# Half sums of the normed features on GpSimd, a fifth seven-product gate tile per FFN layer, and scores issued one head ahead of attention

## The chip, the cores and the metric

The kernel runs on one core of a Trainium2 chip. The metric is device microseconds (us) of one execution; lower is better. The inputs stay in FP32 and every matmul has FP32 accuracy.

## The reference

512 tokens of width 1024 pass through two layers and a last RMSNorm. Cut to what matters:

```python
for layer in range(2):
    h = rms_norm(x, g)
    x = x + (even_mixer(h) if layer % 2 == 0 else odd_mixer(h))
    x = x + mem_cross_attention(rms_norm(x, gx), mem)     # 4 heads, 256 memory tokens
    x = x + (silu(h2 @ w_gate) * (h2 @ w_up)) @ w_down    # h2 = rms_norm(x, gf); 2816 hidden features
return rms_norm(x, g_final)

# even: z = h @ w_in, split in u (512), cq (256), ckv (128), kr (32)
#   pool part: window means of u, minus u, times a 128x128 weight per group
#   attention: 8 heads, q = norm(cq) @ w_q_up, (k, v) = norm(ckv) @ w_kv_up, rope on 32 columns,
#              s = q k^T + causal mask, p = softmax(s), o = p v
#   out = concat(pool, o) @ w_out
# odd: gate, xb = split(h @ w_in); xb = conv4(xb); r, i = sigmoid(xb @ w_r), sigmoid(xb @ w_i)
#   a = exp(-8 r softplus(-lam)); scan h[t] = a h[t-1] + sqrt(1-a^2) i xb; out = (gelu(gate) * h) @ w_out
# cross: k = (norm(mem) * g_m) @ w_k  (rows scaled by 1/rms of each memory token)
```

## The kernel before, in words

Features lie on the 128 partitions, tokens along the free dimension: x is eight tiles of 128x512. Every FP32 operand is split into a high and a low part in fp32r (`split`, L151-161: a copy on ScalarE, L157, then a subtraction on VectorE, L158), and a product is made of three matmuls, wh·xh, wh·xl, wl·xh (`mm3`, L164-173). So one k-block of a 128x512 output is three matmuls of 512 columns, and TensorE (PE) is what the kernel is built around. Weights arrive by DMA in blocks of 512 KB into two buffers, and are split into four buffers of high and four of low parts (L115-117; casts at L102 on ScalarE, L103 on VectorE). Outputs go to eight PSUM banks under four names with two banks each: mm, att, s, tr (L47).

The stages follow each other: setup, even layer, cross attention, FFN, odd layer, cross attention, FFN, tail. Each engine works through its own queue in order; the order in the queues comes from the framework's scheduler, which runs over the whole program. `issue_after` makes an instruction come behind another one in that order.

**Even layer** (L441-650). `qkv_pair(p)` makes q for two heads (bank att, times a rotary row on VectorE, L545, then split) and k. `attend(h, ...)` makes, for one head, four rows of scores in banks s (L581-584, the mask added by a matmul), a softmax per row (`softmax_row`, L652-658: maximum on VectorE, exponential and scaling on ScalarE, into tiles pr), transposes into banks tr (L596), splits them (pth, ptl) and multiplies them with v into a bank att (L611). The pairs are written so that q and k of the next pair stand ahead of both heads of this pair; behind each pair come two tiles of the memory keys of layer 0 (`mem_keys`, named mg, xk in the profile; eight tiles of 24 matmuls of 128x256, L377-386) and one pool tile (evp, pp). The key tile leaves its bank by a VectorE product with the row Rmem (L386). Weights of q, k (evqkv) and v (evv) have three pools of one buffer each, apart from the common ones.

**Odd layer** (L940-1077). Convolution tiles and recurrent gates come first, then the scan on VectorE and ScalarE (`lru_scan`, tiles h). While that runs, PE makes the gate tiles 0 to 3 (odin weights, 24 matmuls of 128x512 each), key tiles 0 to 3 of the memory of layer 1, gate tiles 4 to 7, key tiles 4 to 7, all in the two mm banks. A gate tile leaves its bank by a VectorE product with the row Rrow (L1053), a key tile by one with Rmem (L386).

**FFN** (L770-938). 22 gate tiles f in five parts; when a part is done, its down product is made piece by piece behind the next part's tiles (`down`, bank s, 12 matmuls of 512 columns for four k-blocks; two pieces per tile f, L913-917). In a plain tile f, 8 k-blocks of gate and of up make 48 matmuls of 128x512. The tiles f = 0, 1 use x times its gain and are scaled by the row R behind the product; meanwhile `normed` (L794-803) makes normed features in four buffers (tag sraw), which the plain tiles from f = 2 on use in split form. From f = 5 on a tile is made by `fast` (L819-869): seven products of half sums, of four k-blocks each, make the two 128x512 outputs, 84 matmuls of 128x256. The half sums of the weights (sa, sb, from the raw weights gr) are made per tile on VectorE; those of the features (ta, tb) once per layer in `halves` (L805-817), four operations of 128x256 for each of four k, L810-813, all on VectorE, followed by splits. These use temporaries of tag t2, of which there are two. The raw weights gr of the fast tiles use the same four sraw buffers as the normed features, so the first ones wait for `halves` to have read them.

Of the kernel before, what the change touches and what calls it, by code (L numbers as in the profile page):

```python
# [9 lines left out]
F32 = mybir.dt.float32  # L10
# [4 lines left out]
ALU = mybir.AluOpType  # L15
# [3 lines left out]
P = 128  # L19
T = 512  # L20
D = 1024
KD = D // P
NT = T // P
MEM = 256
# [11 lines left out]
FAST = range(5, 20), range(5, 22)  # L36
# [71 lines left out]
class Trunk:  # L108
# [268 lines left out]
    def mem_keys(self, layer, mg, m0, m1, low=None):  # L377
# [4 lines left out]
        for m in range(m0, m1):  # L382
# [3 lines left out]
            self.nc.vector.tensor_mul(self.keys[:, m, :], ps[:, :MEM], self.Rmem)  # L386
# [54 lines left out]
    def even(self, nrm, nxt_spec):  # L441
# [4 lines left out]
        with ExitStack() as ctx:  # L446
# [8 lines left out]
            wsm = [ctx.enter_context(tc.tile_pool(name=f"evw{i}", bufs=1)) for i in "rhl"]  # L455
# [80 lines left out]
            Wqkv = Weights(self, ins["ev_qkv"], "evqkv", wsm)  # L536
# [32 lines left out]
            def attend(h, q, k, yh, yl):  # L569
                qh, ql = q  # L570
                kh, kl = k
                pr = [pt.tile([P, (i + 1) * P], F32, name=self.nm("pr"), tag=f"pr{i}", bufs=1 if i == 2 else 2) for i in range(NT)]
                for grp in ((0, 1), (2,), (3,)):
# [3 lines left out]
                    for i in grp:  # L577
# [6 lines left out]
                        nc.tensor.matmul(s[:, o + n - P:o + n], self.identb, self.maskb, start=False, stop=True)  # L584
                        reg[i] = r
                        o += n
                    for i in grp:
                        self.softmax_row(reg[i], pr[i])
                tiles = {}
# [17 lines left out]
                for j in range(NT):  # L607
                    vh, vl = (a[:, hp] for a in vs[j])
                    o = ps[:, j * P:]
                    th, tl = tiles[j]  # L610
                    nc.tensor.matmul(o, vh, th, start=j == 0, stop=False)  # L611
                    nc.tensor.matmul(o, vh, tl, start=False, stop=False)
                    nc.tensor.matmul(o, vl, th, start=False, stop=j == NT - 1)
# [10 lines left out]
            def att_pair(p, q, k):  # L624
                y = self.pair(YS)
                for i in range(2):
                    attend(2 * p + i, q[i], k[i], *y)
                y_att.append(y)

# [3 lines left out]
            qkv = qkv_pair(0)  # L633
            for p in range(HEADS // 2):
                q, k = qkv
                if p == 0:
                    v_tiles()
                qkv = qkv_pair(p + 1) if p + 1 < HEADS // 2 else None
                att_pair(p, q, k)
                if p == 0:  # L640
                    mg = self.mem_gained(0, self.xp, "x")
                else:
                    self.mem_keys(0, mg, 2 * p - 2, 2 * p)
                pool_tile(p, us[p])
# [603 lines left out]
```

## Time and profile before

| | |
|---|---|
| time, median of 3 runs | 1379.61 us (1379.57 to 1381.86) |
| profiled execution | 1381.9 us, its span 1379.9 us, mean granted clock 0.992 |
| PE busy | 1354.2 us, 98% of the span |
| VectorE (DVE), ScalarE (ACT) busy | 953.3 us (69%), 665.5 us (48%) |
| GpSimd (POOL) busy | 110.0 us (8%), 122 instructions |
| DMA | 139.41 MB, mean 101 GB/s |

Busy is the sum of the stretches in which at least one instruction of the engine ran. The groups of instructions show the busy time of a group, its mean duration, and the idle time of the engine just before its instructions with what ended it. A group's durations overlap on PE, since matmuls are pipelined; what one costs in the stream is the distance between two starts. PEclk in a window is the granted TensorE clock, 1.00 being full speed. The stretches used below are the even layer's attention (about 56 to 165 us), the FFN of layer 0 around its tiles 3 to 8 (about 356 to 453 us) and the odd layer's gate and key tiles (about 740 to 830 us).

### The profile page before, as it was taken

To read this page: it belongs to the slowest core of one execution; us is meant where nothing else is said; L and a number is where in the kernel's file an instruction comes from. 1 tells how busy PE (TensorE), PEld (TensorE's weight loads), DVE (VectorE), ACT (ScalarE), POOL (GpSimd) and SP (SyncE) were. 2 spreads that over 40 slices of the span, in tenths; PEclk is the share of its full clock that TensorE was granted. 3 is DMA by queue.
4 is the path that set the end of the run, shared out by engine and by line. 5 is a ranking of instruction groups with operands and counts; after the bars stand their busy time and mean duration, and the time that the engine had idled before them with its cause. 6 is when DMAs were issued, how large, how long until landed. Compare 5 with 4: busy or idle time off the path is not lost.

```text
span 1379.9 us, 19407 instructions
## 1 busy us (share of the span) xinstructions
PE 1354.2 (98%) x7640; PEld 1183.3 (86%) x7640; DVE 953.3 (69%) x1488; ACT 665.5 (48%) x1073; POOL 110.0 (8%) x122
## 2 busy tenths in 40 slices
PE   9899999999999999999999989999999999999998
PEld 8678788888889999999888878888888999999987
DVE  7787573455787777777888587435549777777643
ACT  8478653354444444444535655335445344444431
POOL 0231021013000000000110001111120000000001
PEclk9899999999999999999999999999999999999999
DMA  7221262323243323321332334223324223233131
GB/s 248 67 92 41 73 194 81 103 81 103 78 142 107 106 94 98 112 93 43 116 111 83 104 107 139 100 68 92 109 99 142 93 93 108 92 107 108 37 117 62
DMA packets 44971, 139.41 MB, mean 101 GB/s; under 512 B 5584, under 2 KB 9808, under 8 KB 44880
## 3 DMA queue, kind: packets, MB, share of 16 engines
q1 hardware_dynamic: 43440, 136.86, 30.6%
q10 hardware_dynamic: 1440, 1.32, 0.3%
q8 instruction: 60, 0.98, 0.3%
q14 instruction: 31, 0.25, 0.1%
HBM read 135.93 MB, written 2.10 MB: 100 GB/s over the span
## 4 chain that ended last, share of the span: by engine, by line
PE 90%; DVE 5%; ACT 3%; issue 1%; POOL 0%; POOLq 0%; DVEq 0%; ACTq 0%
PE mm L171 15%; PE mm L172 15%; PE mm L173 15%; PE s L171 6%; PE s L173 6%; PE s L172 6%; PE att L171 6%; PE att L172 6%; PE att L173 6%; PE tr L172 1%; PE tr L173 1%; PE tr L171 1%; PE tr L188 1%; DVE xk_l L103 1%; PE att L688 1%
## 5 line engine op out<-in xcount | busy, mean ns | idle before, releaser
L171 PE MATMUL s<-act,dn_h 128*128 128x512 f32 x304 | 119.2, 393 | 0.5 <-DVE x L279 0.5
L172 PE MATMUL s<-act,dn_h 128*128 128x512 f32 x304 | 118.8, 391 | 0.6 <-DVE act L158 0.6
L173 PE MATMUL s<-act,dn_l 128*128 128x512 f32 x304 | 114.6, 393 | 0.0
L157 ACT CAST sw_h<-gr 128x1024 fp32r<-128x1024 f32 x64 | 53.4, 835 | 105.8 <-PE att L172 58.2
L251 POOL TENSOR_TENSOR ssq<-ssq,t 128x512 f32<-128x512 f32 x30 | 50.7, 1690 | 615.1 <-ACT t L250 615.1
L158 DVE TENSOR_TENSOR sw_l<-gr,sw_h 128x1024 fp32r<-128x1024 f32 x64 | 61.3, 958 | 17.6 <-ACT sw_h L157 14.6
L172 PE MATMUL mm<-tb,sw_h 128*128 128x256 f32 x256 | 72.5, 283 | 0.0
L173 PE MATMUL mm<-tb,sw_l 128*128 128x256 f32 x256 | 72.3, 283 | 0.0
L171 PE MATMUL mm<-tb,sw_h 128*128 128x256 f32 x256 | 71.8, 280 | 0.0
L157 ACT CAST sw_h<-sb 128x1024 fp32r<-128x1024 f32 x32 | 33.5, 1048 | 75.4 <-PE s L172 67.8
L171 PEld LDWEIGHTS s<-act,dn_h 128*128 128x128 f32 x304 | 57.3, 189 | 11.3 <-DVE x L279 0.9
L172 PEld LDWEIGHTS s<-act,dn_h 128*128 128x128 f32 x304 | 57.1, 188 | 11.3 <-DVE act L158 1.0
L279 DVE TENSOR_TENSOR x<-s,x 128x512 f32<-128x512 f32 x72 | 49.5, 687 | 23.6 <-PE s L173 23.6
L173 PEld LDWEIGHTS s<-act,dn_l 128*128 128x128 f32 x304 | 57.2, 188 | 10.0
L103 DVE TENSOR_TENSOR dn_l<-dn_raw,dn_h 128x1024 fp32r<-128x1024 f32 (+1 forms) x40 | 46.8, 1171 | 16.0 <-ACT dn_h L102 15.9
L102 ACT CAST dn_h<-dn_raw 128x1024 fp32r<-128x1024 f32 (+1 forms) x40 | 40.3, 1007 | 31.1 <-ACT pc L854 17.0
L279 DVE TENSOR_TENSOR x<-mm,x 128x512 f32<-128x512 f32 x24 | 16.4, 691 | 51.4 <-PE mm L173 51.4
L102 ACT CAST gu_h<-gu_raw 128x1024 fp32r<-128x1024 f32 x24 | 25.3, 1053 | 55.3 <-PE mm L172 37.7
L157 ACT CAST sw_h<-sa 128x1024 fp32r<-128x1024 f32 x32 | 33.6, 1051 | 34.9 <-PE mm L172 33.4
L173 PE MATMUL mm<-act,xq_l 128*128 128x512 f32 x128 | 50.1, 391 | 0.0
L172 PE MATMUL mm<-act,xq_h 128*128 128x512 f32 x128 | 50.0, 390 | 0.0
L171 PE MATMUL mm<-act,xq_h 128*128 128x512 f32 x128 | 49.9, 390 | 0.0
(478 smaller groups left out, 4509.9 us busy)
## 6 DMA issues: line engine op xcount, KB each, us to landing
gr<-in_ffn_gu_dram SPq DMA_DIRECT2D x64, 512.0 KB, 3.5
dn_raw<-in_ffn_down_dram SPq DMA_DIRECT2D x32, 512.0 KB, 3.5
gu_raw<-in_ffn_gu_dram SPq DMA_DIRECT2D x24, 512.0 KB, 3.5
xk_raw<-in_xa_w_k_dram SPq DMA_DIRECT2D x16, 512.0 KB, 3.5
xq_raw<-in_xa_w_q_dram SPq DMA_DIRECT2D x16, 512.0 KB, 3.5
xv_raw<-in_xa_w_v_dram SPq DMA_DIRECT2D x16, 512.0 KB, 3.5
xo_raw<-in_xa_w_o_dram SPq DMA_DIRECT2D x16, 512.0 KB, 3.5
odin_raw<-in_od_w_in_dram SPq DMA_DIRECT2D x16, 512.0 KB, 3.5
```

The source lines that it names most:

```text
L102: nc.scalar.copy(hi, src)
L103: self.low.tensor_sub(lo, src, hi[:, :].bitcast(F32))
L157: a = nc.scalar.copy(hi, src)
L158: b = nc.vector.tensor_sub(lo, src, hi.bitcast(F32))
L171: nc.tensor.matmul(out, wh, xh, start=begin and i == 0, stop=False, **kw)
L172: nc.tensor.matmul(out, wh, xl, start=False, stop=False, **kw)
L173: self.mm_ins = nc.tensor.matmul(out, wl, xh, start=False, stop=end and i == last, **kw).ins
L188: self.sum_ins = nc.tensor.matmul(ps[:, o + t:o + t + 1], a[:, t * P:(t + 1) * P], self.ones[:, 0:1], start=i == 0, stop=i == len(terms) - ...
L251: (low or nc.gpsimd).tensor_add(ssq[:, :n], ssq[:, :n], sq[:, :n])
L279: self.nc.vector.tensor_add(self.x[m], ps, self.x[m] if src is None else src)
L688: nc.tensor.matmul(banks[t], a[:, ts], wh[:, ws], start=k == 0, stop=False)
```

## The change

Five edits come together.

1. `FAST` starts at f = 4 in both layers: one tile per layer goes from plain to fast, and it is the first one that uses the half sums.
2. In `halves` the four operations per k go from VectorE to GpSimd, and b gets the other sign; `fast` makes sb with the other sign to match.
3. Key tiles of layer 1 leave the bank by a copy on ScalarE; the product with Rmem is made in place on VectorE in the cross attention, ahead of the split of that tile.
4. Gate tiles 4 to 7 leave the bank by a copy on ScalarE; the product with Rrow follows in place on VectorE.
5. `attend` is cut in two, `scores` (score matmuls and softmax) and `attend` (transposes, splits, product with v). The scores of head h+1 are issued ahead of `attend` of head h, and the products with v are held behind the last score matmul. The row tile pr2 gets two buffers instead of one, and the evqkv weights use the common weight buffers in place of their own.

```diff
-FAST = range(5, 20), range(5, 22)
+FAST = range(4, 20), range(4, 22)
...
-            self.nc.vector.tensor_mul(self.keys[:, m, :], ps[:, :MEM], self.Rmem)
+            if layer == 0:
+                self.nc.vector.tensor_mul(self.keys[:, m, :], ps[:, :MEM], self.Rmem)
+            else:
+                self.nc.scalar.copy(self.keys[:, m, :], ps[:, :MEM])
...
-            Wqkv = Weights(self, ins["ev_qkv"], "evqkv", wsm)
+            Wqkv = Weights(self, ins["ev_qkv"], "evqkv")
...
-                        nc.tensor.matmul(s[:, o + n - P:o + n], self.identb, self.maskb, start=False, stop=True)
+                        self.score_ins = nc.tensor.matmul(s[:, o + n - P:o + n], self.identb, self.maskb, start=False, stop=True).ins
...
-                for j in range(NT):
...
+                with tc.issue_after(self.score_ins):
+                    for j in range(NT):
...
-            def att_pair(p, q, k):
-                y = self.pair(YS)
-                for i in range(2):
-                    attend(2 * p + i, q[i], k[i], *y)
-                y_att.append(y)
...
+            pair_of(0)
+            v_tiles()
+            pr = scores(0, *heads[0])
+            for h in range(HEADS):
+                p = h // 2
+                if h % 2 == 0:
+                    y = self.pair(YS)
+                    y_att.append(y)
+                    if p + 1 < HEADS // 2:
+                        pair_of(p + 1)
+                nxt_pr = scores(h + 1, *heads[h + 1]) if h + 1 < HEADS else None
+                attend(h, pr, *y)
+                pr = nxt_pr
+                if h % 2:
...
+                    pool_tile(p, us[p])
...
+                key = self.keys[:, m, :]
+                if layer:
+                    nc.vector.tensor_mul(key, key, self.Rmem)
+                self.split(key, h, l)
...
-                nc.vector.tensor_sub(a[:, lo], g[0][:, lo], g[0][:, hi])
-                nc.vector.tensor_sub(a[:, hi], g[1][:, hi], g[0][:, hi])
-                nc.vector.scalar_tensor_tensor(b[:, lo], a[:, lo], -1.0, g[1][:, hi], op0=ALU.mult, op1=ALU.subtract)
-                nc.vector.scalar_tensor_tensor(b[:, hi], b[:, lo], -1.0, g[1][:, lo], op0=ALU.mult, op1=ALU.subtract)
+                nc.gpsimd.tensor_sub(a[:, lo], g[0][:, lo], g[0][:, hi])
+                nc.gpsimd.tensor_sub(a[:, hi], g[1][:, hi], g[0][:, hi])
+                nc.gpsimd.tensor_add(b[:, lo], a[:, lo], g[1][:, hi])
+                nc.gpsimd.tensor_sub(b[:, hi], b[:, lo], g[1][:, lo])
...
-            nc.vector.tensor_add(sb[:, :T], sa[:, :T], w11)
-            nc.vector.tensor_add(sb[:, T:], sb[:, :T], w12)
+            nc.vector.scalar_tensor_tensor(sb[:, :T], sa[:, :T], -1.0, w11, op0=ALU.mult, op1=ALU.subtract)
+            nc.vector.tensor_sub(sb[:, T:], w12, sb[:, :T])
...
-                nc.vector.tensor_mul(t, ps, self.Rrow)
+                if m < KH:
+                    nc.vector.tensor_mul(t, ps, self.Rrow)
+                else:
+                    nc.scalar.copy(t, ps)
+                    nc.vector.tensor_mul(t, t, self.Rrow)
```

The number of PE matmuls goes from 7640 to 7712, 36 more in each FFN layer. The order of the instructions on the engines changes at these places. First the even layer, PE's queue of the kernel before, where the score matmuls of a head (s) end, and its transposes (tr, of the rows pr) and products with v (att from pth, vh) follow; cqh, evqkv is a q tile of the next pair:

```order
383 L583 MATMUL s_1113<-act_100_539,act_93_532 128x384
384 L584 LDWEIGHTS identb
385 L584 MATMUL s_1113<-maskb,identb 128x128
386 L596 MATMUL tr_924<-ident,pr_876 128x128
387 L596 MATMUL tr_933<-ident,pr_876 128x128
388 L611 MATMUL att_949<-pth_929,vh_716 128x512
389 L171 MATMUL att_1054<-cqh_426,evqkv_h_1050 128x512
```

In the changed kernel the same stretch of PE's queue:

```order
383 L603 MATMUL tr_966<-ident,pr_827 128x128
384 L603 MATMUL tr_975<-ident,pr_827 128x128
385 L171 MATMUL mm_1386<-pp_1382,evp_h_657 128x512
386 L172 MATMUL mm_1386<-pp_1383,evp_h_657 128x512
387 L173 MATMUL mm_1386<-pp_1382,evp_l_658 128x512
388 L584 MATMUL s_954<-act_100_530,act_92_522 128x512
389 L585 MATMUL s_954<-act_101_531,act_92_522 128x512
390 L586 MATMUL s_954<-act_100_530,act_93_523 128x512
391 L587 LDWEIGHTS identb
392 L587 MATMUL s_954<-maskb,identb 128x128
393 L619 MATMUL att_991<-pth_971,vh_707 128x512
```

The last row of scores and a pool tile now stand between the last transposes of a head and its product with v.

Second the odd layer, DVE's queue of the kernel before, at the first key tile (the product into keys at L386), in the middle of the scan (h, i):

```order
890 L1040 SCALAR_TENSOR_TENSOR h_7171<-t_1261_8154,h_7171 128x512
891 L103 TENSOR_TENSOR xk_l_7861<-xk_raw_7858,xk_h_7860 128x1024
892 L386 TENSOR_TENSOR keys_6780<-mm_7768,Rmem 128x256
893 L1040 SCALAR_TENSOR_TENSOR h_7214<-t_1262_8158,h_7214 128x512
894 L1044 TENSOR_TENSOR i_7288<-h_7128,i_7288 128x512
```

In the changed kernel that bank is emptied from ACT's queue (L389), where the table load of the square roots, square roots (L1012), squares (L1057) and the cast of a gate weight (odin_h) stand ahead of it:

```order
631 L1012 ACT_TABLE_LOAD
632 L1012 ACTIVATE h_7176<-h_7176 128x512
633 L1057 ACTIVATE t_1278_8214<-r_7396 128x512
634 L1012 ACTIVATE h_7219<-h_7219 128x512
635 L102 CAST odin_h_7940<-odin_raw_7938 128x1024
636 L389 COPY keys_6828<-mm_7816 128x256
637 L1057 ACTIVATE t_1279_8218<-r_7509 128x512
638 L1012 ACTIVATE h_7262<-h_7262 128x512
639 L389 COPY keys_6828<-mm_7848 128x256
```

The emptying of the first key tile has moved from behind a weight split on DVE to behind the table load, three instructions of the scan and a weight cast on ACT. The sixteen operations of `halves` in a layer now stand as one run in POOL's queue.

More of the change, by code (lines that the diff above doesn't have):

```diff
@@ L454, in even @@
             pt = ctx.enter_context(tc.tile_pool(name="evpt", bufs=2))
-            wsm = [ctx.enter_context(tc.tile_pool(name=f"evw{i}", bufs=1)) for i in "rhl"]
             z, zins = self.z, self.mm_ins
@@ L567, in v_tiles, with scores @@
                     vs.append((h, l))
-            def attend(h, q, k, yh, yl):
+            def scores(h, q, k):
                 qh, ql = q
                 kh, kl = k
-                pr = [pt.tile([P, (i + 1) * P], F32, name=self.nm("pr"), tag=f"pr{i}", bufs=1 if i == 2 else 2) for i in range(NT)]
+                pr = [pt.tile([P, (i + 1) * P], F32, name=self.nm("pr"), tag=f"pr{i}", bufs=2) for i in range(NT)]
                 for grp in ((0, 1), (2,), (3,)):
@@ L588, in attend @@
                         self.softmax_row(reg[i], pr[i])
+                return pr
+            def attend(h, pr, yh, yl):
                 tiles = {}
@@ L606, in attend @@
                 hp = slice(h // 2 * P, (h // 2 + 1) * P)
-                for j in range(NT):
[L608 to L613, printed above, removed]
+                with tc.issue_after(self.score_ins):
+                    for j in range(NT):
+                        vh, vl = (a[:, hp] for a in vs[j])
+                        o = ps[:, j * P:]
+                        th, tl = tiles[j]
+                        nc.tensor.matmul(o, vh, th, start=j == 0, stop=False)
+                        nc.tensor.matmul(o, vh, tl, start=False, stop=False)
+                        nc.tensor.matmul(o, vl, th, start=False, stop=j == NT - 1)
                 rs = slice((h % 2) * VD, (h % 2 + 1) * VD)
@@ L632, in even, with pair_of @@
             wph, wpl = Weights(self, ins["ev_pool"], "evp").get(0)
[L633 to L644, printed above, removed]
+            heads = []
+            def pair_of(p):
+                q, k = qkv_pair(p)
+                heads.extend(zip(q, k))
+            pair_of(0)
[12 more added lines that the diff above has]
+                if h % 2:
+                    if p == 0:
+                        mg = self.mem_gained(0, self.xp, "x")
+                    else:
+                        self.mem_keys(0, mg, 2 * p - 2, 2 * p)
+                    pool_tile(p, us[p])
             self.mem_keys(0, mg, 6, KD)
@@ L674, in k_tile @@
                 l = kvp.tile([P, MEM], F32R, name=self.nm("kl"), tag=f"kl{m}")
-                self.split(self.keys[:, m, :], h, l)
+                key = self.keys[:, m, :]
+                if layer:
+                    nc.vector.tensor_mul(key, key, self.Rmem)
+                self.split(key, h, l)
                 return h, l
@@ L1052, in gate_tile @@
                 t = self.actp.tile([P, T], F32, name=self.nm("g"), tag=f"act{other}")
-                nc.vector.tensor_mul(t, ps, self.Rrow)
+                if m < KH:
+                    nc.vector.tensor_mul(t, ps, self.Rrow)
+                else:
+                    nc.scalar.copy(t, ps)
+                    nc.vector.tensor_mul(t, t, self.Rrow)
                 return t
```

## The prediction

> **What bounds the kernel now.** I read the page first, then the groups of instructions with the idle time in front of them, then windows and the timeline around each edited place. From the page:
>
> ```profile
> PE 1354.2 (98%) x7640; PEld 1183.3 (86%) x7640; DVE 953.3 (69%) x1488; ACT 665.5 (48%) x1073; POOL 110.0 (8%) x122
> PE 90%; DVE 5%; ACT 3%; issue 1%; POOL 0%; POOLq 0%; DVEq 0%; ACTq 0%
> ```
>
> PE is busy for 98% of the span and holds 90% of the chain that ended last. So the change can gain in three ways only: fewer matmul columns, fewer waits of PE, and less time at a reduced clock behind such waits. The groups on PE whose idle time the edits touch (the last columns: busy time and mean ns, then idle time before, by releaser):
>
> ```profile
> L171 PE MATMUL mm<-act,odin_h 128*128 128x512 f32 x112 | 44.5, 398 | 3.5 <-DVE g L1053 2.8 <-DVE keys L386 0.7
> L171 PE MATMUL mm<-mg,xk_h 128*128 128x256 f32 x128 | 36.9, 288 | 1.9 <-DVE keys L386 1.9
> L596 PE MATMUL tr<-ident,pr 128*128 128x128 f32 x80 | 16.1, 279 | 2.0 <-ACT pr L658 1.6 <-DVE ptl L158 0.3
> L611 PE MATMUL att<-pth,vh 128*128 128x512 f32 x8 | 3.6, 444 | 2.4 <-ACT pth L157 2.4
> L581 PE MATMUL s<-act,act 128*128 128x512 f32 x8 | 3.4, 431 | 0.7 <-ACT pr L656 0.5
> ```
>
> Three stages are edited, and PE's idle time in their edited waits is about 5 us in the odd layer, 5 us at the heads of the attention, and two waits at its beginning.
>
> **FFN: a fast tile for f = 4.** The windows give one plain tile (48 matmuls of 512 columns) and one fast tile with its two down pieces (84 of 256 columns and 24 of 512); after start, end and length come the busy times of PE, PEld, DVE, ACT and POOL, then PEclk:
>
> ```profile
> 391.10:402.00 10.90, 10.90 (x50) 9.03 (x49) 9.60 (x16) 4.63 (x8) 0.00 (x0) 1.00 0.58 188
> 437.10:452.70 15.60, 15.60 (x110) 14.58 (x109) 12.20 (x17) 6.95 (x10) 0.00 (x0) 1.00 0.30 102
> ```
>
> 10.90 / 48 = 0.227 us per 512-column matmul. The fast tile alone is 15.60 − 24 × 0.227 = 10.15 us. So each layer saves 10.90 − 10.15 = 0.75 us, two layers **1.5 us**, if the half sums are there in time. They come from Pool now. The timeline has the normed features and before's last TB split:
>
> ```profile
> 360.90 5.39 DVE L799 SCALAR_TENSOR_TENSOR xn<-x,vecs,R 128x512 f32<-128x512 f32 x8
> 399.92 0.69 DVE L158 TENSOR_TENSOR tb<-t,tb 128x512 fp32r<-128x512 f32 x1
> ```
>
> and the groups with Pool's nearest operations, and VectorE's one that is replaced:
>
> ```profile
> L251 POOL TENSOR_TENSOR ssq<-ssq,t 128x512 f32<-128x512 f32 x30 | 50.7, 1690 | 615.1 <-ACT t L250 615.1
> L548 POOL TENSOR_TENSOR act<-t,act 128x512 fp32r<-128x512 f32 x6 | 7.9, 1318 | 38.6 <-ACT act L547 38.6
> L1097 POOL TENSOR_TENSOR t<-t,t 128x384 f32<-128x384 f32 x6 | 6.1, 1013 | 326.9 <-ACT t L1095 326.9
> L810 DVE TENSOR_TENSOR t<-xn 128x256 f32<-128x256 f32 x8 | 3.3, 418 | 0.0
> ```
>
> No row has Pool at 256 columns. The two quicker rows differ by 305 ns for 128 columns, 2.38 ns per column, which puts 256 columns at 0.71 us; half of the slowest row gives 0.85. Before's last TB split ran at 399.92, which was early enough, since the first fast tile began at 402.0. Now it begins at 391.1. Its products run X·f1 and Y·f2 first, from features that are ready long before; with 12 matmuls of 10.15 / 84 = 0.121 us a product is 1.45 us, so TA is needed from 394.0 and TB from 395.5. Pool can begin after the fifth of the eight normed tiles, 360.9 + 5 × 0.67 = 364.3. It makes a and b of one k in 4 × 0.71 = 2.9 us, and must then wait until VectorE has split them, because there are two t2 buffers. VectorE still has the weight splits of f = 2, 3 and 5 to do between. Walking the new orders of VectorE and Pool row by row, the last TA is split at about 387 and the last TB at about 392: 7 and 4 us ahead of need. What hides the sixteen operations is thus 27 us of plain tiles; if VectorE fell 4 us behind, every further us would come straight out of the 1.5. Bounds of the term: 1.5 down to −2.5 (the cover gone by 2 us in each layer). I take 1.5. The Trainium skill, "GPSIMD Engine Reference", section 4.1 on engine selection, advises VectorE for ordinary elementwise work, with Pool about half as fast; that agrees with 0.71 against 0.418 here, and by the rule the edit is a loss if it matters at all, which is the third rival.
>
> In the fast tiles sb costs nothing: DVE is busy 12.20 of 15.60 there.
>
> **Odd layer: banks emptied by ScalarE.** The timeline of before where the four odin and key tiles meet:
>
> ```profile
> 784.75 0.28 PE L171 MATMUL mm<-mg,xk_h 128*128 128x256 f32 x1
> 795.12 0.36 PE L171 MATMUL mm<-mg,xk_h 128*128 128x256 f32 x1 [1.57 <-DVE keys L386]
> 798.97 0.47 PE L171 MATMUL mm<-act,odin_h 128*128 128x512 f32 x1 [0.75 <-DVE keys L386]
> 818.36 0.47 PE L171 MATMUL mm<-act,odin_h 128*128 128x512 f32 x1 [2.78 <-DVE g L1053]
> 825.49 0.28 PE L171 MATMUL mm<-mg,xk_h 128*128 128x256 f32 x1
> ```
>
> and the window behind its last wait:
>
> ```profile
> 815.00:826.00 11.00, 8.22 (x32) 6.41 (x31) 7.62 (x10) 2.70 (x4) 0.00 (x0) 0.84 0.47 144
> ```
>
> The three waits are 1.57 + 0.75 + 2.78 = 5.1 us. Behind the last one, 24 matmuls took 825.49 − 818.36 = 7.13 us where 24 × 0.227 = 5.45 is usual, at a granted clock of 0.84 in that window: about 1.65 more. Price of what is touched: 6.75 us. The release by VectorE goes, because it came late there: scans of h fill its queue. What is late next is ScalarE:
>
> ```profile
> 788.53 1.28 ACT L994 ACT_TABLE_LOAD   x1
> 789.83 0.63 ACT L994 ACTIVATE h<-h 128x512 f32<-128x512 f32 x1
> 790.36 0.62 ACT L1039 ACTIVATE t<-r 128x512 f32<-128x512 f32 x1
> 790.88 0.62 ACT L994 ACTIVATE h<-h 128x512 f32<-128x512 f32 x1
> 791.41 1.03 ACT L102 CAST odin_h<-odin_raw 128x1024 fp32r<-128x1024 f32 x1
> 789.16 0.42 DVE L386 TENSOR_TENSOR keys<-mm,Rmem 128x256 f32<-128x256 f32 x1
> ```
>
> with a copy of that size from the groups:
>
> ```profile
> L854 ACT COPY pc<-mm 128x256 f32<-128x256 f32 x32 | 11.7, 365 | 2.0 <-PE mm L173 2.0
> ```
>
> In the new order the copy of the first key tile stands behind just these five ACT instructions. The first bank was free at 789.58 before; now the copy starts behind the cast, at 791.41 + 1.03 = 792.4, and ends near 792.75 (0.365 for one of 128x256). The third key tile takes that bank. It began without a wait at 795.12 − 1.57 − 2.9 = 790.65 (the fourth tile's start, less its wait, less the 24 × 0.121 us of the third), so it would now wait about 2.1 us. The later copies follow in an ACT queue with more slack; I allow 0.75 in all, for a cast that waits for its DMA ahead of one copy. So the term is 6.75 − 2.1 − 0.75 = **3.8 us**. Bounds: 2.3, if the new wait brings a slow clock as the 2.78 one did (−1.5), and 5.0 if ACT runs ahead of the walk. The product in place adds 8 × 0.42 us to VectorE in the cross attention, and 4 × 0.68 behind gate tiles; neither holds a bank of PE. Behind the latter wait the gelus, which come after the whole scan in ACT's queue.
>
> **Even layer: scores a head ahead.** Its beginning:
>
> ```profile
> 65.27 0.68 DVE L545 TENSOR_TENSOR t<-att,ropeC 128x512 f32<-128x512 f32 x1
> 66.00 0.50 PE L171 MATMUL att<-evv_h,ckh 128*128 128x512 f32 x1 [2.83 <-DVE t L545]
> 69.41 0.47 PE L582 MATMUL s<-act,act 128*128 128x128 f32 x1 [1.33 <-DVE act L158]
> 57.99 1.21 DVE L103 TENSOR_TENSOR xk_l<-xk_raw,xk_h 128x1024 fp32r<-128x1024 f32 x1
> ```
>
> and the window behind the first wait:
>
> ```profile
> 66.00:76.00 10.00, 8.18 (x28) 5.72 (x28) 7.69 (x17) 4.33 (x8) 3.57 (x3) 0.66 0.36 111
> ```
>
> The first wait, 2.83 us, is for the rotary product that empties the bank of head 1's q. In VectorE's new order one xk split (1.21) leaves the way to it and two operations of 0.68 (a split of evv's weight and one of a pool tile) come in: 0.15 us later. The second wait, 1.33, loses about 1.0: the splits of 1.21 and 0.68 that stood ahead of the low half of k are gone, and one of about 0.8 is new. The waits at the heads are those of the groups above: L596 for pr 1.6, L611 for pth 2.4, L581 for pr 0.5, together 4.5. In the new order 12 score matmuls of the next head, and often a pool or key tile, stand ahead of the transposes; head 7 has no next head, and the ends of pairs were already filled by q and key tiles. I take two thirds, 3.0. Sum: 3.0 + 1.0 − 0.15 = **3.85 us**. Bounds: 7.05 if all 4.5 go and half of the 3.4 us that a clock of 0.66 costs in 10 us goes too; −1.0 if the shared weight buffers cost a cast and a split, 1.05 + 1.21, once or twice on the path. The 1.05 is the cast of a 128x1024 weight:
>
> ```profile
> L102 ACT CAST gu_h<-gu_raw 128x1024 fp32r<-128x1024 f32 x24 | 25.3, 1053 | 55.3 <-PE mm L172 37.7
> ```
>
> **Sum**: 1.5 + 3.8 + 3.85 = 9.15 us. The profiled execution is 1381.9 us (span 1379.9 and 2.0 outside it), 2.3 above the median of 1379.61; it would come to 1372.8, and the median to 1370.5 us. About 0.2%, 2.8 us, is what a measurement can tell from no change: faster is below 1376.9, slower above 1382.4.
>
> **The rivals.**
>
> *The attention gains only at its beginning.* Before's PE order already lets the scheduler put q tiles and key tiles between the products with v, so what waits at the heads may be the softmax chain itself, maximum to exponential to scale, which is as long in the new order. For it: ACT ends 2.4 + 1.6 of these waits and stays as loaded. Against it: the scores now come a whole head earlier. Even gives 1.0 in place of 3.85: 1373.3.
>
> *The new key copy wait brings a slow clock.* A wait of 2.83 was followed by a window at 0.66, one of 2.78 by 0.84; the one of 1.57 was not. The new one, 2.1, lies between. Price 1.5: 1372.0. The Trainium skill, "TensorE: Matmul & The Clock Gate", Part 1, has the clock fall only after an idle window of about 3.4 us; the two waits here were shorter, so the measurement decides, and by the page this rival would not exist.
>
> *The half sums on Pool lie on the path.* If PE waits for TA and TB at f = 4, the sixteen operations cost 16 × (0.71 − 0.418) = 4.7 us a layer, 9.3 in two: 1379.8, no change. Against it stands the slack of 4 us in the walk.
>
> *The weight buffers starve the key tiles (slower).* evqkv and evv take places in the common high and low buffers, of which there are four, while pool weights hold one for the whole attention. If two q, k weights are held at once, key tiles get one buffer, and each waits for its cast and split behind the tile before, 1.05 + 1.21 = 2.26 us. Their raw blocks take turns in the two raw buffers as well, and SP issues the DMAs in order. Over the six key tiles inside the attention: 13.6 us, 1370.5 + 13.6 = 1384.1. It turns the sign from (1379.6 − 1370.5) / 6 = 1.5 us per tile, and passes 1382.4 from 2.0. Against it: a q, k weight is read by 15 matmuls and is then free, and VectorE and ACT have idle time in the attention.
>
> **How the numbers follow.** My forecast 0.50, first rival 0.17, second 0.10, third 0.07, fourth 0.06; the remaining 0.10 is better than forecast, the slow clock at the attention's beginning gone too (−3.4, 1367.1). The range 1364.5 to 1377.0 takes in the sum of the upper bounds (7.05 − 3.85 and 5.0 − 3.8 give 4.4; with the other half of that clock, 1.7, it is 6.1) and of the lower ones (2.3 and −1.0 in place of 3.8 and 3.85 give 6.35). Faster 0.85: all of forecast, first, second and better, less 0.02 for two lower bounds at once; same 0.09; slower 0.06.
>
> **What would show it.** Right: in the changed profile no wait of PE on L1053's bank from gate tile 4 on; a wait of about 2 us, released by ACT's copy, at the third key tile of layer 1; the first fast tile of a layer in about 10.15 us with no idle time in front of the TA and TB products; less than 2 us of idle time at the transposes and products with v. Wrong: idle time of PE behind Pool or a TB split near 394; waits at mg, xk tiles in the attention, released by xk casts or splits; a granted clock below 0.9 in other stretches than before.

## The result, and the profile after

The changed kernel takes 1390.26 us (median of 4 runs, 1389.09 to 1391.59); beside it the kernel before took 1380.48 (1379.57 to 1381.86). The ratio is 1.0067, with a 95% interval of 1.0055 to 1.0080: slower, where 1370.5 was forecast and 1377.0 was the upper end of the range. The profiled execution has 1391.14 us and a span of 1389.4, 9.5 us more than before's profiled one.

The first matmul with the weights of each stage, in the timelines of the two profiles, gives the length of the stages (us). "FFN 1" ends here where its plain tile f = 20 begins.

| stage | before | changed | difference | predicted |
|---|---|---|---|---|
| even, first evqkv to first xq | 153.8 | 154.1 | +0.3 | −3.85 |
| FFN 0, first gu to first odin | 346.1 | 351.2 | +5.1 | −0.75 |
| odd, first odin to first odout | 145.2 | 143.7 | −1.5 | −3.8 |
| FFN 1, first gu to f = 20 | 294.0 | 298.9 | +4.9 | −0.75 |

The rest of the 9.5 is −0.5 ahead of the even layer, +0.1 in the cross attention and +1.1 at the very end, nearly all behind the last instruction that issues an output DMA.

The engines' row of the changed kernel's page (compare 1354.2, 953.3, 665.5 and 110.0 before):

```profile
PE 1356.1 (98%) x7712; PEld 1190.1 (86%) x7712; DVE 964.6 (69%) x1476; ACT 675.5 (49%) x1095; POOL 153.4 (11%) x154
```

Pool has 43 us more for 32 operations, where 32 × 0.71 = 23 were reckoned. VectorE is busy for 11 us more: the two fast tiles give it sums and splits, but 32 operations of 0.42 us have left it. The groups on PE that answer to those shown of before, with the idle time in front of them:

```profile
L171 PE MATMUL mm<-act,odin_h 128*128 128x512 f32 x112 | 43.7, 390 | 0.0
L171 PE MATMUL mm<-mg,xk_h 128*128 128x256 f32 x128 | 38.4, 300 | 9.0 <-DVE act L161 5.0 <-ACT keys L389 2.1 <-ACT g L1074 1.9
L603 PE MATMUL tr<-ident,pr 128*128 128x128 f32 x80 | 15.0, 282 | 1.8 <-ACT pr L673 1.2 <-DVE ptl L158 0.6
L619 PE MATMUL att<-pth,vh 128*128 128x512 f32 x8 | 3.9, 486 | 0.0
L584 PE MATMUL s<-act,act 128*128 128x512 f32 x8 | 3.5, 438 | 0.0
```

The waits that the change is aimed at are gone: 3.5 to 0 at gate tiles, 2.4 to 0 at the product with v, 2.0 to 1.8 at the transposes. In their place the key tiles wait 9.0 us instead of 1.9, for three releasers that before did not have. And a new place waits, the first fast tile of each FFN layer; PE's timeline of layer 0:

```profile
396.05 0.38 PE L171 MATMUL mm<-tb,sw_h 128*128 128x256 f32 x1 [0.64 <-ACT pc L872]
398.10 0.39 PE L172 MATMUL mm<-tb,sw_h 128*128 128x256 f32 x1 [0.59 <-DVE tb L158]
400.90 0.50 PE L171 MATMUL s<-act,dn_h 128*128 128x512 f32 x1 [2.30 <-ACT dn_h L102]
```

and the windows around them (columns as above: PE, PEld, DVE, ACT, POOL busy, PEclk, DMA):

```profile
391.00:402.00 11.00, 7.48 (x53) 6.67 (x52) 11.00 (x16) 6.11 (x11) 2.73 (x3) 0.98 0.39 119
402.00:407.00 5.00, 5.00 (x28) 4.69 (x27) 4.11 (x7) 1.68 (x2) 0.00 (x0) 0.70 0.47 161
```

PE idles 3.5 of 11 us there, VectorE not at all (11.00 of 11.00), and behind it the clock is at 0.70 for 5 us (3.4 us at 0.50, so 1.7 us lost). These two make up about the 5.1 us of FFN 0: the 0.75 that the fast tile saves is used up by matmuls that start at longer distances just behind each wait (0.8 in all). TB is late, and the casts that follow are late with it. How the half sums ran, from Pool's timeline:

```profile
373.56 3.53 POOL L828 TENSOR_TENSOR t<-xn 128x256 f32<-128x256 f32 x1 [5.37 <-DVE ta L158]
377.05 2.38 POOL L829 TENSOR_TENSOR t<-xn 128x256 f32<-128x256 f32 x1
379.39 0.73 POOL L830 TENSOR_TENSOR t<-t,xn 128x256 f32<-128x256 f32 x1
381.37 1.19 POOL L828 TENSOR_TENSOR t<-xn 128x256 f32<-128x256 f32 x1
384.48 0.75 POOL L831 TENSOR_TENSOR t<-t,xn 128x256 f32<-128x256 f32 x1
...
388.26 1.12 POOL L828 TENSOR_TENSOR t<-xn 128x256 f32<-128x256 f32 x1 [3.04 <-DVE ta L158]
389.35 1.72 POOL L829 TENSOR_TENSOR t<-xn 128x256 f32<-128x256 f32 x1
391.81 1.60 POOL L830 TENSOR_TENSOR t<-t,xn 128x256 f32<-128x256 f32 x1 [0.74 <-DVE tb L158]
393.49 1.06 POOL L831 TENSOR_TENSOR t<-t,xn 128x256 f32<-128x256 f32 x1
```

and from VectorE's and ScalarE's:

```profile
388.71 1.76 DVE L158 TENSOR_TENSOR sw_l<-gr,sw_h 128x1024 fp32r<-128x1024 f32 x1
390.99 0.67 DVE L158 TENSOR_TENSOR tb<-t,tb 128x512 fp32r<-128x512 f32 x1
392.73 1.23 DVE L158 TENSOR_TENSOR ta<-t,ta 128x512 fp32r<-128x512 f32 x1
397.37 0.68 DVE L158 TENSOR_TENSOR tb<-t,tb 128x512 fp32r<-128x512 f32 x1
...
399.28 0.62 ACT L157 CAST act<-t 128x512 fp32r<-128x512 f32 x1 [3.28 <-DVE t L893]
399.80 1.04 ACT L102 CAST dn_h<-dn_raw 128x1024 fp32r<-128x1024 f32 x1
```

With VectorE idle beside it an operation takes 0.73 to 0.75 us, as the sum had it (0.71). Beside a working VectorE it takes 1.06 to 1.21, and up to 3.53 where VectorE runs splits and one product without a pause, each in its usual 0.68. VectorE pays too: a split of 0.67 takes 1.23, one of 1.21 takes 1.76. The Trainium skill, "SBUF — State Buffer", section "Who interferes with whom", says that a VectorE instruction with two inputs in SBUF contends with a GpSimd instruction that reads SBUF, through a shared read interface; this trace agrees: thirteen of the sixteen operations of layer 0 are lengthened, VectorE's own beside some of them too, with the prices given here.

The last TB split ends at 398.05 where the walk had 392. Two in-order queues carry this on: VectorE's product for tile f = 3 (L893) stands behind that split, ScalarE's cast of that product behind it, and the cast of the down weights behind that, so the down product waits 2.30 us for an engine that was idle for 3.28.

### The profile page after: what moved, and what is told of

Read it like the earlier page. It is cut to its first block, busy times and chain, and to the rows that moved or that the text cites. A ratio compares the mean times of both kernels' runs of the same rounds, so it can differ in the third digit from the quotient of the medians.

```text
span 1389.4 us, 19596 instructions
## 1 busy us (share of the span) xinstructions
PE 1356.1 (98%) x7712; PEld 1190.1 (86%) x7712; DVE 964.6 (69%) x1476; ACT 675.5 (49%) x1095; POOL 153.4 (11%) x154
## 5 line engine op out<-in xcount | busy, mean ns | idle before, releaser
L157 ACT CAST sw_h<-gr 128x1024 fp32r<-128x1024 f32 x68 | 56.7, 834 | 102.6 <-PE att L172 55.3
L172 PE MATMUL mm<-tb,sw_h 128*128 128x256 f32 x272 | 77.2, 284 | 1.2 <-DVE tb L158 1.2
L158 DVE TENSOR_TENSOR sw_l<-gr,sw_h 128x1024 fp32r<-128x1024 f32 x68 | 66.2, 973 | 17.4 <-ACT sw_h L157 14.1
L171 PE MATMUL mm<-tb,sw_h 128*128 128x256 f32 x272 | 76.5, 281 | 1.1 <-ACT pc L872 1.1
L173 PE MATMUL mm<-tb,sw_l 128*128 128x256 f32 x272 | 76.9, 283 | 0.0
L171 PEld LDWEIGHTS mm<-tb,sw_h 128*128 128x128 f32 x272 | 51.7, 190 | 1.6 <-ACT pc L872 1.5
L172 PEld LDWEIGHTS mm<-tb,sw_h 128*128 128x128 f32 x272 | 51.0, 188 | 1.7 <-DVE tb L158 1.6
L173 PEld LDWEIGHTS mm<-tb,sw_l 128*128 128x128 f32 x272 | 51.1, 188 | 0.0
```

Of the source, the lines that this page charges most:

```text
L157: a = nc.scalar.copy(hi, src)
L158: b = nc.vector.tensor_sub(lo, src, hi.bitcast(F32))
L171: nc.tensor.matmul(out, wh, xh, start=begin and i == 0, stop=False, **kw)
L172: nc.tensor.matmul(out, wh, xl, start=False, stop=False, **kw)
L173: self.mm_ins = nc.tensor.matmul(out, wl, xh, start=False, stop=end and i == last, **kw).ins
```

## The experiments

Stages of the runs, in us as in the table above, with times and ratios to the kernel before on the same chip. A dash is a stage that the run does not edit.

| run | even | FFN 0 | odd | FFN 1 | median us | ratio (95% interval) |
|---|---|---|---|---|---|---|
| f4_only | – | 347.1 | – | 295.1 | 1384.38 | 1.0021 (1.0009 to 1.0033) |
| pool_halves_only | – | 346.1 | – | 294.0 | 1381.42 | 1.0003 (0.9993 to 1.0012) |
| two_k_on_gpsimd | – | 349.1 | – | 296.7 | 1385.07 | 1.0032 (1.0021 to 1.0044) |
| early_tile_third_buffer | – | 351.8 | – | 297.8 | 1392.83 | 1.0098 (1.0080 to 1.0116) |
| attn_only | 153.5 | – | – | – | 1380.87 | 0.9998 (0.9989 to 1.0008) |
| attn_own_weights | 151.7 | – | – | – | 1377.97 | 0.9982 (0.9972 to 0.9992) |
| changed_own_weights | 151.7 | 351.2 | 143.9 | 300.3 | 1389.05 | 1.0054 (1.0038 to 1.0070) |
| key_copies_only | – | – | 142.5 | – | 1378.34 | 0.9987 (0.9977 to 0.9998) |
| gate_copies_only | – | – | 142.0 | – | 1378.37 | 0.9981 (0.9972 to 0.9991) |
| without_ffn_edits | 151.7 | – | 142.1 | – | 1373.80 | 0.9959 (0.9945 to 0.9973) |
| first_key_on_vector | 150.2 | – | 139.4 | – | 1372.17 | 0.9935 (0.9921 to 0.9948) |

The unedited stages tell how far a stage can be trusted: the FFN layers lay within 0.1 us of 346.1 and 294.0 in every run that left them alone; the odd layer came out at 145.0 to 145.2 or at 143.6, the even layer at 153.8 in before and 155.2 to 156.0 in six runs. The steps are stretches in which PE runs at half clock (granted clock 0.50), as the last section shows. So in the even and odd columns a difference of 1.7 or 3.4 us can be the clock alone.

**f4_only: the early tile without Pool.**

```diff
-FAST = range(5, 20), range(5, 22)
+FAST = range(4, 20), range(4, 22)
```

> The kernel before with the first edit alone: f = 4 becomes a fast tile in both layers, the half sums stay on VectorE. Theory A (VectorE's queue is what is late at f = 4: in about 385 to 402 us it was busy for 11.00 of 11.00 us, because the sums and the splits of the first fast tiles' weights fall on the end of the half sums, and GpSimd only makes it a little worse): PE waits at the first fast tile of each layer here too, 3 us or more with a slow clock behind it, and each FFN layer gets longer than in the kernel before, by 2 to 7 us; total 1384 to 1394. Theory B (the half sums are late because GpSimd is slow, 1.06 to 3.53 us an operation): with VectorE's 0.42 the TA and TB products do not wait, each layer gets 0.75 shorter; total about 1379.

FFN 0 took 347.1 and FFN 1 295.1, 1.0 and 1.1 above before. TB does not make PE wait in f = 4, though its last split ran as late as 401.42 (this FFN begins 1.6 us later than the changed kernel's); here the scheduler has put the last three TB matmuls behind a product and 20 matmuls of the down pieces. VectorE's split and PE's next wait in the two timelines:

```profile
401.42 0.68 DVE L158 TENSOR_TENSOR tb<-t,tb 128x512 fp32r<-128x512 f32 x1
...
398.71 0.29 PE L173 MATMUL mm<-tb,sw_l 128*128 128x256 f32 x1
404.82 0.28 PE L171 MATMUL mm<-tb,sw_h 128*128 128x256 f32 x1
405.94 0.39 PE L171 MATMUL mm<-act,sw_h 128*128 128x256 f32 x1 [0.57 <-ACT sw_h L157]
```

What is left is a ripple of small waits (0.57, 0.22, 0.23) at the second fast tile, whose weights are split late; with the matmuls that start late just behind them (0.8 in all) they cost 1.8, less the saving of 0.75. So each theory gets a part: theory B is right that Pool makes most of the loss (5.1 and 4.9 against 1.0 and 1.1), theory A that the early tile loses even without it. The saving of 0.75 is there (48 matmuls of 0.227 go, 84 of 0.12 come), but it is used up.

**pool_halves_only: Pool without the early tile.**

```diff
-                nc.vector.tensor_sub(a[:, lo], g[0][:, lo], g[0][:, hi])
+                nc.gpsimd.tensor_sub(a[:, lo], g[0][:, lo], g[0][:, hi])
...
```

> The kernel before with the second edit alone: half sums on GpSimd, fast tiles from f = 5 as before. Theory A: the sixteen operations have 16 us more until the first fast tile needs them, and VectorE has 16 x 0.42 = 6.7 us less to do; no wait of PE at the first fast tile, the time as before within 0.1% (1379 to 1381). Theory B, if GpSimd is so slow that it is late even then: waits at the first TA or TB product, 1 to 4 us a layer, total 1382 to 1388.

346.1 and 294.0, as before, with no wait at the first fast tile. Pool's operations are just as long as in the changed kernel:

```profile
374.60 3.54 POOL L810 TENSOR_TENSOR t<-xn 128x256 f32<-128x256 f32 x1 [5.37 <-DVE ta L158]
380.43 0.74 POOL L812 TENSOR_TENSOR t<-t,xn 128x256 f32<-128x256 f32 x1
394.52 1.07 POOL L813 TENSOR_TENSOR t<-t,xn 128x256 f32<-128x256 f32 x1
```

So neither edit alone explains the loss: 0.0 for one, 1.0 for the other, 5.1 for both. Sixteen us more cover hide the slow operations altogether. VectorE's busy time shows what they cost it:

```profile
PE 1353.6 (98%) x7640; PEld 1183.2 (86%) x7640; DVE 952.1 (69%) x1456; ACT 665.7 (48%) x1073; POOL 152.5 (11%) x154
```

It lost 32 operations of 0.42 us, 13.4 in all, and got 1.2 us back (953.3 to 952.1).

**two_k_on_gpsimd: half of the half sums on Pool.**

```diff
-                nc.vector.tensor_sub(a[:, lo], g[0][:, lo], g[0][:, hi])
+                eng = nc.gpsimd if k < 2 else nc.vector
+                eng.tensor_sub(a[:, lo], g[0][:, lo], g[0][:, hi])
...
```

> The first and second edits (fast tile at f = 4), but GpSimd makes the half sums of k = 0 and 1 only and VectorE those of k = 2 and 3. Theory H (what is late is the second half of GpSimd's run, which lies beside VectorE's full queue at 380 to 398 us, where both engines slow each other): each FFN layer is between 0.75 us below and 1.1 us above before (346.1 and 294.0 us), as with all half sums on VectorE, instead of 5.1 and 4.9 above; total 1379 to 1383. Theory I (any half sums on GpSimd make VectorE's operations beside them long, 1.23 for 0.68, and that alone makes the first fast tile late): 2 us or more above before in each layer, total 1384 to 1390.

2.9 and 2.7 above before: theory I by the number, though the run does not separate longer operations from the new order of the queues. The loss of FFN 0 grows with the operations on Pool: 1.0 with none, 2.9 with eight, 5.1 with sixteen, of which 1.7 is the half clock that neither of the others has; 3.4 without it. PE now waits for TA as well as TB:

```profile
394.05 0.38 PE L172 MATMUL att<-ta,sw_h 128*128 128x256 f32 x1 [0.99 <-DVE ta L158]
397.03 0.39 PE L171 MATMUL mm<-tb,sw_h 128*128 128x256 f32 x1 [0.48 <-ACT tb L157]
404.59 0.38 PE L171 MATMUL mm<-act,sw_h 128*128 128x256 f32 x1 [0.67 <-ACT sw_h L157]
```

**early_tile_third_buffer: a buffer more between the two engines.**

```diff
-                a, b = self.tmp("t2"), self.tmp("t2")
+                a, b = self.tmp("t2"), st.tile([P, T], F32, name=self.nm("t"), tag="th", bufs=1)
```

> The first and second edits (fast tile at f = 4, half sums on GpSimd), with a buffer of its own for b beside the two t2 temporaries for a, so that GpSimd can go on with the next k while VectorE splits the last. In the changed kernel GpSimd waited 5.4, 3.0 and 0.7 us a layer for VectorE's splits of ta and tb, and its sixteen operations took 21.4 us. Theory G (the waits between the two engines make the half sums late): the last TB split comes 2 us or more earlier, the waits of 0.6 + 0.6 + 2.3 us at the first fast tile shrink to under 1 us, and an FFN layer is back at the 346.1 us of before or below. Theory B (each operation is long because VectorE works at the same time, 1.06 to 3.53 us against 0.73 alone): the waits shrink by less than half, each FFN layer stays 2 us or more above before; total 1384 to 1390.

Theory G falls: 5.7 (with 1.7 of half clock) and 3.8 (with none) above before; the total, 1392.83, is even above theory B's 1384 to 1390. The last TB split came at 395.57, 0.9 us earlier than in the changed kernel when both are counted from the first gu matmul, and PE waited longer, 3.62 us. The reason is in ScalarE's queue:

```profile
394.92 0.62 ACT L157 CAST tb<-t 128x512 fp32r<-128x512 f32 x1 [2.50 <-POOL t L813]
398.10 0.62 ACT L157 CAST act<-t 128x512 fp32r<-128x512 f32 x1 [2.04 <-DVE t L875]
398.62 0.37 ACT L854 COPY pc<-mm 128x256 f32<-128x256 f32 x1
```

PE needed the copy pc (L854), which empties the bank for the TB product. It stood behind a cast that waited for VectorE, which itself had waited 1.28 us for ScalarE's cast of the late half sum. The late half sum had itself taken 3.38 us on Pool. So a late Pool operation held up both in-order queues, and what PE missed is a copy that has nothing to do with half sums.

**attn_only: scores a head ahead.** The fifth edit alone, cut to its core:

```diff
-            Wqkv = Weights(self, ins["ev_qkv"], "evqkv", wsm)
+            Wqkv = Weights(self, ins["ev_qkv"], "evqkv")
...
+                nxt_pr = scores(h + 1, *heads[h + 1]) if h + 1 < HEADS else None
+                attend(h, pr, *y)
```

> The kernel before with the fifth edit alone, scores a head ahead and evqkv weights in the common buffers. Both theories: the even layer as in the changed kernel, where it took 0.3 us longer than before from the first evqkv matmul to the first cross-attention matmul, with waits of about 1.6 and 3.4 us at key tiles for a bank that a pool tile holds (released by VectorE's split of the pool tile, which comes behind ScalarE's, which stands behind a weight cast that waits for its DMA); total 1380 to 1381.5. If the even layer is 2 us or more shorter here, those waits are due to something that the other edits move.

The even layer took 153.5, with waits of 1.43 and 3.42 at key tiles, and the time is the same as before. The changed kernel's timelines show what they are, PE's, ScalarE's and VectorE's:

```profile
143.05 0.58 PE L171 MATMUL mm<-mg,xk_h 128*128 128x256 f32 x1 [3.42 <-DVE act L161]
...
136.85 1.05 ACT L102 CAST evout_h<-evout_raw 128x1024 fp32r<-128x1024 f32 x1 [1.77 <-DMA evout_raw<-in_ev_w_out_dram]
140.94 0.67 ACT L160 ACTIVATE act<-mm,vecs 128x512 fp32r<-128x512 f32 x1
...
142.25 0.74 DVE L161 SCALAR_TENSOR_TENSOR act<-mm,vecs,act 128x512 fp32r<-128x512 f32 x1
```

A pool tile's product ended at 139.0 in one of the two mm banks. ScalarE had waited 1.77 us for an output weight and then worked through its queue; the copy that empties the bank came at 140.94, VectorE's half at 142.25. Behind this wait PE runs at half clock for 6.8 us, 3.4 us lost, in the changed kernel and in attn_only alike (window of the changed kernel):

```profile
142.20:148.90 6.70, 5.85 (x24) 5.14 (x24) 3.40 (x9) 4.26 (x11) 0.00 (x0) 0.50 0.25 81
```

**attn_own_weights: the same, with the weight buffers as they were.**

```diff
-            Wqkv = Weights(self, ins["ev_qkv"], "evqkv")
+            Wqkv = Weights(self, ins["ev_qkv"], "evqkv", wsm)
```

> As the run with the fifth edit alone, but the evqkv weights keep their own three buffers, as in the kernel before. Theory C (the shared weight buffers make the evqkv, key and output weights wait for each other, so that the casts of key and output weights stand waiting for DMA in ScalarE's queue, ahead of the copies that empty the banks): the waits of 1.6 and 3.4 us at key tiles go and the even layer is 4 to 6 us shorter than before, total 1374 to 1377. Theory D (the wait comes from the new order itself: the softmax of the next head stands ahead of the pool tile's split, whatever the buffers): key tiles wait by 2 us or more again, and the total stays within 2 us of the kernel before.

Theory C by its sign: both waits go, and the layer is at 151.7, 2.1 below before's profile. That is less than the 4 to 6 expected, and the total of 1377.97 lies above 1374 to 1377: a wait of 1.69 for the low part of a transposed row comes up at 98.11, with 3.4 us of half clock behind it. Against the six unedited executions at 155.2 to 156.0 the layer is 3.5 to 4.3 shorter.

**changed_own_weights: the same line changed in the whole changed kernel.**

```diff
-            Wqkv = Weights(self, ins["ev_qkv"], "evqkv")
+            Wqkv = Weights(self, ins["ev_qkv"], "evqkv", wsm)
```

> The whole changed kernel, but the evqkv weights keep their own three buffers. Theory C (the shared buffers cost the waits of 1.6 and 3.4 us at key tiles): the even layer takes about 151.7 us, as in the run of the fifth edit with own weights, instead of 154.1, and the total falls by about 2.4 us to 1387 to 1388.5. Rival: if the even layer stays above 153.5, the gain seen there came from the order of that kernel and not from the buffers.

151.7 again, from 154.1, the figure expected. Of these 2.4 us 1.7 are the clock: 13.7 us of the layer ran at half clock in the changed kernel, 10.2 here. The total, 1389.05, is above the 1387 to 1388.5 that was said; in the profiled execution FFN 1 took 300.3, with 6.8 us at half clock behind its first fast tile instead of 3.4.

**key_copies_only and gate_copies_only: the odd layer's two edits apart.** First the key tiles of layer 1 (with the product later, in the cross attention):

```diff
+                self.nc.scalar.copy(self.keys[:, m, :], ps[:, :MEM])
```

> The kernel before with the third edit alone: key tiles of layer 1 copied from their banks by ScalarE, gate tiles 4 to 7 still emptied by VectorE. The odd layer (first odin matmul to first odout matmul) took 145.2 us before and 143.7 in the changed kernel. Theory E (each bank's wait moves from one full queue to the other): the waits of 1.57 and 0.75 go, one of about 2.1 at the third key tile, released by ScalarE's copy, comes, and the 2.78 at a gate tile with its slow clock stays: odd layer 144.8 to 145.5, total unchanged. Rival F (the key copies are a clear gain): odd layer under 144.

then the gate tiles 4 to 7:

```diff
-                nc.vector.tensor_mul(t, ps, self.Rrow)
+                if m < KH:
+                    nc.vector.tensor_mul(t, ps, self.Rrow)
+                else:
+                    nc.scalar.copy(t, ps)
+                    nc.vector.tensor_mul(t, t, self.Rrow)
```

> The kernel before with the fourth edit alone: gate tiles 4 to 7 copied from their banks by ScalarE, key tiles still emptied by VectorE. Theory E: the waits of 1.57 and 0.75 at key tiles stay, the 2.78 and the slow clock behind it (1.65) go, and a new wait of about 1.9 comes at the key tile that needs the bank of gate tile 7, because that copy stands behind the cast of a key weight that waits for its DMA: odd layer 145.2 - 4.43 + 1.9 = 142.7, total 1377 to 1378.5. Rival F (the gate copies gain nothing): odd layer 144.5 or more.

Both gain: 142.5 and 142.0, rival F for the keys and slightly more than theory E said for the gates. Neither has a stretch of half clock, so the unedited layer to compare with is the one of 143.6: the gains are 1.1 and 1.6. With the key copies the gate wait did not stay at 2.78; it shrank to 1.33 + 0.26. VectorE's queue is shorter by the key products there, which is argued and not tested. With the gate copies the new wait was 0.82 and not 1.9.

**without_ffn_edits and first_key_on_vector.** The third to fifth edits with own evqkv weights; the second also gives the first key tile back to VectorE:

```diff
-            if layer == 0:
+            if layer == 0 or m == 0:
                 self.nc.vector.tensor_mul(self.keys[:, m, :], ps[:, :MEM], self.Rmem)
...
-                if layer:
+                if layer and m:
                     nc.vector.tensor_mul(key, key, self.Rmem)
```

> Third, fourth and fifth edits, with own buffers for the evqkv weights, and no FFN edit: fast tiles from f = 5, half sums on VectorE. If the stages add up, the even layer is 2.1 us shorter than before (as in the run with own weights) and the odd layer 1.5 us (as in the changed kernel): 3.6 us in all, total 1376 to 1377. If the odd edits gain nothing on their own, 1378.

> The third, fourth and fifth edits with own evqkv weights and no FFN edit, as before, but the first key tile of layer 1 is emptied by VectorE again, since ScalarE's copy of it stands behind the table load. Theory E (the third key tile waits 2.08 us for that copy alone): this wait goes, at most 0.7 us comes at the fourth key tile, the odd layer falls from 142.1 to about 140.5 us; total 1372 to 1375. Rival: if VectorE's scan queue makes that bank late again, a wait of 1 us or more stays and the odd layer is at 141.5 or above.

The first is at 151.7 and 142.1, 1373.8 us in all, below the 1376 to 1377 expected, since the odd layer gave 3.1 us where 1.5 was reckoned. The second removes the wait behind the table load; PE's rows at the waiting key tile, of the first and then of the second kernel:

```profile
790.50 0.38 PE L171 MATMUL mm<-mg,xk_h 128*128 128x256 f32 x1 [2.08 <-ACT keys L389]
```

```profile
789.92 0.39 PE L171 MATMUL mm<-mg,xk_h 128*128 128x256 f32 x1 [0.25 <-ACT keys L389]
```

The odd layer falls to 139.4, and the kernel to 1372.17 us, ratio 0.9935: faster than both the kernel before and the changed one. In the odd layer's 2.7 us, PE's idle time falls by 1.3, and the half clock that followed the wait of 2.08 in the first kernel is gone, another 1.7; 0.3 is lost elsewhere. So more than half of this last step, as profiled, is clock. The even layer, the same in both, differs by 1.5 for the same reason: the wait of 1.69 is in both, the half clock behind it in the first alone.

## Why the prediction was wrong

**FFN term (+10.0 instead of −1.5): the step that failed is the price and the cover of the half sums.** The prediction priced an operation at 0.71 us from two rows, one with VectorE idle beside it and one with VectorE busy for part of the time, and put the last TB split at 392, 4 us ahead of need; it ended at 398.05. It also read the first fast tile of before as beginning at 402.0, where the down pieces begin; that tile began at 407.35, so the edit calls for the half sums 16 us earlier and not 11. The 0.71 holds only with VectorE idle. Beside VectorE, where nearly all of them run, they took 1.06 to 3.53, sixteen in 21.4 us instead of 11.4, and lengthened VectorE's own operations beside them by 3.4 us in layer 0 and 4.6 in layer 1 (each against the median of its kind). The third rival had the half sums on the path, with a chance of 0.07 and a price of 4.7 us a layer; it came to 4.1 and 3.8 over the same tile without Pool. That these lie close is luck: the rival charged all sixteen operations at 0.71, while the measured figure is made of longer operations that are mostly covered, of waits behind them, and of 1.7 us of half clock. Its total came out at no change only because it was counted off the other gains. The range left out the lower bound of −2.5 that the term itself was given, and −10.0 lies far below that too. That the saving of 0.75 per tile would show was wrong as well: even with VectorE's half sums the layer lost 1.0, by waits for late casts and splits of the weights at the second fast tile.

**Even layer (+0.3 instead of −3.85): the head waits were right, the lead-in was not, and a new wait was missed.** Idle time in the named groups fell from 5.1 to 1.8, 3.3 us where 3.0 were forecast. The first wait was to grow by 0.15 and went from 2.83 to 2.98. The second was to fall by 1.0 and fell by 0.1. What was missed is 5.0 us at key tiles and the half clock behind the longest of these waits, 3.4 us more. That the layer is only 0.3 longer has a gain on the other side that the forecast did not have either: the stage less its idle time and its lost clock went from 139.4 to 135.5, since transposes, scores and products with v follow each other more closely where the rows count no idle time. The fourth rival named the shared weight buffers as the danger, but by another way, as casts and splits of the key weights; it was the pool tile's bank, emptied late by ScalarE and VectorE.

**Odd layer (−1.5 instead of −3.8).** The new wait at the third key tile was forecast at 2.1 and measured 2.08. The 0.75 allowed for later copies was too little: gate tile 7's copy stood behind the cast of a key weight that waited 2.33 us for its DMA.

```profile
828.69 1.04 ACT L102 CAST xk_h<-xk_raw 128x1024 fp32r<-128x1024 f32 x1 [2.33 <-DMA xk_raw<-in_xa_w_k_dram]
829.64 0.58 ACT L1074 COPY g<-mm 128x512 f32<-128x512 f32 x1
```

PE waited 1.89 us at 830.27 for it. The clock in the next 5 us was 0.66, 1.7 us lost, so the slow clock that was to go with the 2.78 wait came back with this one. The idle time of the layer fell by 1.1 (5.1 to 4.0) and the clock loss not at all. In the run without the FFN edits the wait at the same place was 0.17, but not because the bank was free sooner: that cast of a key weight began 131.9 us after the layer's first matmul in the changed kernel and 131.7 there. PE came 1.5 us later, since there the half clock had already followed the wait of 2.08.

What stays open: how much of Pool's 4 us a layer is the length of its operations, and how much the scheduler's order, which puts the TB product right behind TA with Pool and partly behind the down pieces with VectorE. No run held that order fixed. Also open is why a wait is followed by half clock in one execution and not in another.

## What to carry to other kernels

Work moved to an idle engine is priced from a row in which its neighbour is busy, not from one in which it runs alone: here 1.06 to 3.53 us for 0.73, and 1.23 for 0.67 on the neighbour. Before a bank is given to another engine, read what stands ahead of the emptying instruction in that engine's queue, above all casts that wait for a DMA and table loads, since an in-order engine that is idle half of the time can be the late one. An edit that needs data earlier takes away the cover of every step that makes them, so these two are tried together and apart.

## What the runs showed of the hardware

From the even layer to the last matmul, wherever the clock of these thirteen traces is reduced, it is at 0.50 for 3.4 or 6.8 us, so that such a stretch costs 1.7 or 3.4 us; a window of 0.66 or 0.89 is one of these and full clock around it. Waits of nearly the same length were followed by such a stretch in some executions and not in others. Behind the 2.78 to 2.80 us at a gate tile the 15 us from 815 on had a granted clock of 0.89 before, and 1.00 in pool_halves_only:

```profile
815.00:830.00 15.00, 12.22 (x65) 10.41 (x64) 11.41 (x16) 6.70 (x10) 0.00 (x0) 0.89 0.41 122
```

```profile
815.00:830.00 15.00, 12.20 (x75) 10.71 (x74) 13.07 (x19) 7.34 (x11) 0.00 (x0) 1.00 0.44 140
```

That is the step between 145.2 and 143.6 for an unedited odd layer. In the unedited even layer it is one stretch more than in before's 153.8, for example in f4_only:

```profile
163.30:166.60 3.30, 3.13 (x10) 2.85 (x11) 1.79 (x4) 0.79 (x2) 0.00 (x0) 0.50 0.02 5
```

In the changed kernel the wait of 2.08 before 797.7 was followed by a full clock and the one of 1.89 before 830.3 was not:

```profile
797.00:805.00 8.00, 7.28 (x55) 7.04 (x56) 8.00 (x12) 7.00 (x14) 0.00 (x0) 1.00 0.22 76
830.00:835.00 5.00, 4.73 (x27) 4.73 (x28) 5.00 (x8) 4.35 (x9) 0.00 (x0) 0.66 0.41 113
```

In without_ffn_edits the wait of 2.08 at the same key tile was followed by half clock:

```profile
791.30:794.60 3.30, 3.30 (x17) 3.30 (x17) 3.30 (x5) 2.45 (x5) 0.00 (x0) 0.50 0.32 104
```

So length alone does not decide. The Trainium skill, "TensorE: Matmul & The Clock Gate", Part 1, has a window of about 3.4 us that runs freely, so that the phase of a wait within it matters; these pairs fit that, while the idle window of 3.4 us that it wants before the clock falls is longer than the 1.89 and 2.78 us that were followed by it here. A single profiled execution thus carries 1.7 or 3.4 us for some waits that need not be the change's, and in the forecast the 1.65 of slow clock in the odd layer should have been a chance and not a certain gain.
